# One PSUM pool of eight named banks for a whole retention-and-pooling trunk, in place of pools opened and closed by each stage

## The chip, the core and the metric

The kernel runs on one core of a Trainium2 chip. TensorE (PE in the profile) multiplies matrices and leaves its sums in PSUM, which has eight banks of 512 fp32 columns by 128 partitions here. VectorE (DVE) and ScalarE (ACT) read PSUM and work in SBUF, GpSimd (POOL) does little in this kernel, and SyncE (SP) issues the weight transfers. The metric is the device time of one execution in microseconds (us): the median of three runs.

## The reference, cut to what matters

The trunk has two layers on a sequence of 256 tokens of width 2048, both of the form h + layer(rms_norm(h)), and a last RMS norm.

```
def retention_layer(x, g_norm, w_in, gn, w_out):        # layer 0
    p = rms_norm(x, g_norm) @ w_in                       # 2048 -> 12288
    q, k, v, z = jnp.split(p, [...], axis=-1)            # 8 heads, 256 / 256 / 512 / 512 wide
    q, k = rope(q), rope(k) * 256 ** -0.5
    o = chunkwise_retention(q, k, v)                     # causal, decayed, chunks of 128
    o = group_norm_per_head(o) * gn * jax.nn.silu(z)
    return o @ w_out                                     # 4096 -> 2048

def pooling_layer(x, g_norm, w_in, w_grp, b_grp, scale, w_out):   # layer 1
    u, z = jnp.split(rms_norm(x, g_norm) @ w_in, [4096], axis=-1) # 2048 -> 8192
    mix = causal_window_mean(u, windows=(2, 4, 8, 16)) - u        # 4 groups of 1024
    mix = (einsum('bsgc,gcd->bsgd', mix, w_grp) + b_grp) * scale
    return (mix * jax.nn.silu(z)) @ w_out                         # 4096 -> 2048
```

## The kernel before

All matrices are fp32, and every product is made of three: each operand is cut into a high part (a cast by ACT, line 91) and a low part (source minus high, by DVE, line 92), and TensorE sums high x high, high x low and low x high. A transfer brings one unit of weights (1 MB, tag `raw`, three buffers); `weights` cuts it into two pairs (tag `w`, five buffers), each pair with a high and a low half of 1024 columns.

The work falls into four stages, one after the other in the program:

- the **first stage** (lines 186 to 353), retention: eight heads with four groups for q and k (`acc`), scores (`sc`), v (`accv`), outputs (`po`), a column sum (`tot`) and four groups for the gate (`acc`, then `gz`). A group of `stationary` is 16 pairs of matmuls, line 122 (512 columns) and line 123 (256 columns). `joined` adds the two halves of the bank (ACT copy, line 131, DVE add, line 132);
- **way 1** (lines 387 to 479, called at line 518), the output projection of retention: for each half of the columns 16 units of weights go into eight sums in eight banks, `c11` to `c22` and the Strassen products `p1`, `p5`, `p6`, `p7`. The four units at the start of a half are plain ones (24 matmuls of line 363 each), so the first Strassen unit comes after 96 matmuls `c`. The last sums are added to the residual `xn` (line 408), and `turn` transposes the new columns by TensorE (`turned`, line 510) and cuts them into `hs2` (lines 96 and 97) for the next stage;
- the **second stage** (lines 551 to 598), pooling: for each of four windows eight groups for u, eight for the gate (`acc` from `hs2`) and eight half groups with `pool_grp` (`acc` from `ms`), each of the latter read by ACT (line 590) and DVE (line 592) and cut into `gs`. At its start `spread_norm` makes the norm's reciprocal on DVE (lines 147 to 163 and 534) and spreads it with two matmuls `tot` (line 139);
- **way 2** (line 645), the output projection of pooling, as way 1 but with the last norm as its tail.

A list scheduler sets the order of the instructions on each engine; it sees which tile holds which bank. Each engine then runs its instructions in that order, and waits at the front one. In the kernel before, each stage opens its own PSUM pools and closes them at its end:

```
        with tc.tile_pool(name=f"{name}_acc", bufs=3, space=bass.MemoryType.PSUM) as acc:
            with tc.tile_pool(name=f"{name}_ret", bufs=5, space=bass.MemoryType.PSUM) as rest:
```

The first and the second stage take three banks for `acc` and five for the rest; each of way 1 and way 2 takes a pool of eight tags, one per sum. A pool that opens gets banks of the pools that were closed, and its first tile comes after the last reading of their tiles.

Of the kernel before, what the change touches and what calls it, by code (L numbers as in the profile page):

```python
# [7 lines left out]
F32 = mybir.dt.float32  # L8
# [5 lines left out]
P = 128  # L14
D = 2048
S = 256
# [14 lines left out]
CLASSIC = ((0, 0), (0, 1), (1, 0), (2, 0), (3, 0), (1, 1), (4, 0), (5, 0), (2, 1), (3, 1), (4, 1), (5, 1))  # L31
FIRST = (20, 16)


# [11 lines left out]
def kernel(  # L46
# [30 lines left out]
    ev = ctx.enter_context(tc.tile_pool(name="ev", bufs=2))  # L77
    psum = []

    @contextmanager  # L80
    def banks(name):

        with tc.tile_pool(name=f"{name}_acc", bufs=3, space=bass.MemoryType.PSUM) as acc:
            with tc.tile_pool(name=f"{name}_ret", bufs=5, space=bass.MemoryType.PSUM) as rest:
                psum[:] = acc, rest
                yield

# [46 lines left out]
    def column_sums(sums):  # L134

        sp = ev.tile([P, 2, S], F32R, tag="sp", name="sp", bufs=1)
        split(sp[:, 0], sp[:, 1], sums)
        tot = psum[1].tile([P, 512], F32, tag="ret", name="tot")
        nc.tensor.matmul(tot[:, :S], ones, sp[:, 0], start=True, stop=False)
        nc.tensor.matmul(tot[:, :S], ones, sp[:, 1], start=False, stop=True)  # L140
        return tot[:, :S]
# [42 lines left out]


    with banks("first"), tc.tile_pool(name="rt", bufs=1) as rt:

        cold = psum[1].tile([P, 512], F32, tag="ret", name="cold")
        for _ in range(9):
# [5 lines left out]
        qk = rt.tile([P, 4, S], F32, tag="qk", name="qk")  # L195
        accs = [psum[0].tile([P, 512], F32, tag="acc", name="acc") for _ in range(3)]
        accs.append(psum[1].tile([P, 512], F32, tag="ret", name="acc"))
        for u in range(4):
# [7 lines left out]
            for i in range(2):  # L206
# [33 lines left out]
        nc.vector.tensor_tensor(out=rpr, in0=rp, in1=wide(rs, 2), op=ALU.mult)  # L240
        rst = psum[1].tile([P, 512], F32, tag="ret", name="rst")
        rsn = rt.tile([P, 2], F32, name="rsn")
# [4 lines left out]
        os = act.tile([P, VT, 2, S], F32R, tag="os", name="os")  # L247
        unit = 4
        for h in range(NH):
# [3 lines left out]
            for c in range(4 if h else 0):  # L253
                blocks = blocks_of(weights(ret_in[unit]))
                unit += 1
                acc = psum[0].tile([P, 512], F32, tag="acc", name="acc")
                stationary(acc, blocks, hs)
                joined(qk[:, c], acc)
# [12 lines left out]
            tc.keep_in_program_order(nc.gpsimd.dma_start(out=mk, in_=masks[h]))  # L271
            sc = psum[1].tile([P, 2, S], F32, tag="ret", name="sc")
            n = 0
# [4 lines left out]
            n = 0  # L278
# [12 lines left out]

            accv = [psum[0].tile([P, 512], F32, tag="acc", name="accv") for _ in range(2)]
            for c in range(4):
# [24 lines left out]
            for c in range(4):  # L318
                cs = slice(c * P, (c + 1) * P)
                po = psum[1].tile([P, 512], F32, tag="ret", name="po")  # L320
# [17 lines left out]
            for c in range(4):  # L338
                blocks = blocks_of(weights(ret_in[unit]))
                unit += 1  # L340
                acc = psum[0].tile([P, 512], F32, tag="acc", name="acc")
# [13 lines left out]
    class Sum:  # L355


        def __init__(self, pool, name, n):
            self.tile, self.n, self.done = pool.tile([P, 512], F32, tag=name, name=name), n, 0

# [25 lines left out]

    def way_out(A, src, first, forms, tmp, pool, work, order, y, after, ends=False):

# [7 lines left out]
        for p in range(2):  # L396
            plain = len(CLASSIC) // 2 * 12
            sums = {}
            for name in order:
                n = 0 if name == "c22" else 3 * NS  # L400
                sums[name] = Sum(pool, name, n + (plain if name[0] == "c" else 0))
            out_of = {(t, c): sums[f"c{t + 1}{c + 1}"] for t in range(2) for c in range(2)}
# [14 lines left out]
            for n, kind in enumerate(ORDER):  # L417
# [16 lines left out]
                b = raw.rearrange("p (m f) -> p m f", m=4)  # L434
# [46 lines left out]
    with tc.tile_pool(name="pl", bufs=1) as pl:  # L481
# [8 lines left out]

        with (
            tc.tile_pool(name="way1", bufs=1, space=bass.MemoryType.PSUM) as way,
            tc.tile_pool(name="work1", bufs=1) as work,
        ):
# [45 lines left out]
        gs = act.tile([P, VT, 2, S], F32R, tag="os", name="gs")  # L540
# [10 lines left out]
        for g, win in enumerate(WINDOWS):  # L551
# [3 lines left out]
            for c in range(GT):  # L555
                blocks = blocks_of(weights(pool_in[2 * GT * g + c]))
                acc = psum[0].tile([P, 512], F32, tag="acc", name="acc")
                stationary(acc, blocks, hs2)
# [17 lines left out]
            for c in range(GT):  # L576
                blocks = blocks_of(weights(pool_in[2 * GT * g + GT + c]))
                acc = psum[0].tile([P, 512], F32, tag="acc", name="acc")
                stationary(acc, blocks, hs2)
                joined(gz[:, c], acc)  # L580
                nc.vector.tensor_tensor(out=gz[:, c], in0=gz[:, c], in1=rs, op=ALU.mult)
                nc.scalar.activation(gz[:, c], gz[:, c], AF.Silu)
            for c in range(GT // 2):
                halves = weights(pool_grp[GT // 2 * g + c])
                for i in range(2):
                    e = GT * g + 2 * c + i
                    acc = psum[0].tile([P, 512], F32, tag="acc", name="acc")
                    stationary(acc, blocks_of(halves[i : i + 1]), ms)
# [48 lines left out]

        with (
            tc.tile_pool(name="way2", bufs=1, space=bass.MemoryType.PSUM) as way,
            tc.tile_pool(name="work2", bufs=1) as work,  # L640
        ):
            tmp = act.tile([P, 4 * S + 2 * P + 512], F32, tag="hs", name="tmp")
            forms = pl.tile([P, NS, 4, 2, P], F32R, tag="ms", name="forms")
            order = ("p1", "p5", "p6", "c11", "c21", "c12", "c22", "p7")
            way_out(gs, pool_out, FIRST[1], forms, tmp, way, work, order, stream, norm, True)

# [110 lines left out]
```

## Time and profile before

| | before |
|---|---|
| median of three runs | 1393.86 us (1393.78 to 1394.25) |
| the profiled execution | 1391.64 us |
| its span | 1389.5 us |
| PE busy | 1364.1 us, 98% of the span |
| DVE busy | 1060.9 us, 76% |
| ACT busy | 719.7 us, 52% |
| POOL busy | 25.4 us, 2% |
| mean granted TensorE clock | 0.99 of full speed |

The profile is that of one execution; its span runs from the first to the last instruction, and the execution's own time is 2.1 us longer. Busy times are those of the engine's instructions. The starts of the rows are what a sum of work can be read from, since matmuls overlap each other and the duration of one is longer than the distance to the next. The stages can be told apart by the tile names: the first stage ends at 576.5 us, way 1 runs from 577.6 to 751 us, the second stage from 755.7 to 1202.7 us, and way 2 from 1207.5 us.

### The profile page before, as it was taken

The numbers are of one execution on the slowest core, as the hardware profiler recorded it, in microseconds if no ns is written. First come the engines' busy times: TensorE is split into PE (matmuls) and PEld (weight loads), VectorE is DVE, ScalarE is ACT, GpSimd is POOL, SyncE is SP. The second block draws the span as 40 slices with busy tenths as digits, with TensorE's granted clock in tenths as the row PEclk, the third lists the DMA queues.
The fourth block names the chain that finished last, engine by engine and source line by source line (L and its number), as shares of the span: only waits on it lengthen the run. The fifth ranks groups of instructions, "written<-read, shape, count | busy, mean of one in ns | idle before, by whom it ended". The sixth has DMA issues, their size and how long they took to land.

```text
span 1389.5 us, 18380 instructions
## 1 busy us (share of the span) xinstructions
PE 1364.1 (98%) x7176; PEld 1171.6 (84%) x7176; DVE 1060.9 (76%) x1545; ACT 719.7 (52%) x1027; POOL 25.4 (2%) x33
## 2 busy tenths in 40 slices
PE   8999999999999999999998999999999999899997
PEld 7888888888888888888887888888888888788885
DVE  6886868686868686898777867876886896868676
ACT  6455545455545454555454455455545545545443
POOL 0000000000000000000000000000000000000102
PEclk8999999999999999999999999999999999999999
DMA  8545454545555545475555555555555555446552
GB/s 298 209 161 197 172 191 177 190 179 188 182 187 180 184 173 190 153 261 196 182 189 180 195 199 182 185 199 195 183 188 191 198 185 185 179 164 230 182 210 93
DMA packets 39493, 262.66 MB, mean 189 GB/s; under 512 B 4512, under 2 KB 4896, under 8 KB 9072
## 3 DMA queue, kind: packets, MB, share of 16 engines
q1 hardware_dynamic: 37872, 255.93, 52.0%
q0 software_dynamic: 1536, 5.57, 1.1%
q8 instruction: 56, 0.92, 0.3%
q14 instruction: 29, 0.24, 0.0%
HBM read 259.39 MB, written 2.10 MB: 188 GB/s over the span
## 4 chain that ended last, share of the span: by engine, by line
PE 96%; DVE 2%; ACT 1%; issue 1%; DMA 1%; SPq 0%; DVEq 0%; ACTq 0%
PE acc L122 37%; PE c L363 21%; PE acc L123 19%; PE accv L302 4%; PE accv L304 4%; PE accv L303 4%; PE p L363 3%; PE po L322 1%; DVE w L92 1%; DMA xin<-in_xT 1%; PE po L324 1%; PE sc L276 0%; DVE hs L97 0%; PE sc L281 0%; ACT w L91 0%
## 5 line engine op out<-in xcount | busy, mean ns | idle before, releaser
L92 DVE TENSOR_TENSOR w<-raw,w 128x1024 fp32r<-128x1024 f32 x472 | 568.1, 1209 | 168.0 <-ACT w L91 160.0
L122 PE MATMUL acc<-hs,w 128*128 128x512 f32 x1984 | 692.4, 392 | 3.5 <-DVE rs_t L161 3.5
L91 ACT CAST w<-raw 128x1024 fp32r<-128x1024 f32 x472 | 486.9, 1038 | 305.0 <-PE acc L123 130.7
L123 PE MATMUL acc<-hs,w 128*128 128x256 f32 x1984 | 556.1, 280 | 0.0
L122 PEld LDWEIGHTS acc<-hs,w 128*128 128x128 f32 x1984 | 372.0, 187 | 84.7 <-issue 3.7
L123 PEld LDWEIGHTS acc<-hs,w 128*128 128x128 f32 x1984 | 375.5, 189 | 1.0
L363 PE MATMUL c<-w,gs 128*128 128x512 f32 x624 | 149.3, 394 | 4.6 <-DVE m L592 4.6
L131 ACT COPY hl<-acc 128x256 f32<-128x256 f32 x128 | 47.9, 374 | 199.5 <-PE acc L123 197.0
L363 PE MATMUL c<-w,os 128*128 128x512 f32 x624 | 149.3, 391 | 0.9 <-DVE gz L132 0.9
L363 PEld LDWEIGHTS c<-w,gs 128*128 128x128 f32 x624 | 118.7, 190 | 30.6 <-issue 4.9
L363 PEld LDWEIGHTS c<-w,os 128*128 128x128 f32 x624 | 116.6, 188 | 26.1 <-DVE gz L132 1.2
L302 PE MATMUL accv<-w,hs 128*128 128x512 f32 x256 | 99.8, 390 | 1.2 <-DVE qk L132 1.2
L303 PE MATMUL accv<-w,hs 128*128 128x512 f32 x256 | 99.8, 390 | 0.0
L304 PE MATMUL accv<-w,hs 128*128 128x512 f32 x256 | 99.7, 390 | 0.0
L122 PE MATMUL acc<-ms,w 128*128 128x512 f32 x256 | 90.6, 397 | 0.0
L123 PE MATMUL acc<-ms,w 128*128 128x256 f32 x256 | 72.0, 281 | 0.0
L91 ACT CAST w<-s 128x1024 fp32r<-128x1024 f32 x32 | 33.6, 1050 | 52.0 <-PE c L363 43.9
L122 PEld LDWEIGHTS acc<-ms,w 128*128 128x128 f32 x256 | 48.1, 188 | 11.8
L92 DVE TENSOR_TENSOR w<-s,w 128x1024 fp32r<-128x1024 f32 x32 | 39.2, 1224 | 24.4 <-ACT w L91 24.4
L302 PEld LDWEIGHTS accv<-w,hs 128*128 128x128 f32 x256 | 48.1, 188 | 11.1 <-DVE qk L132 1.5
L304 PEld LDWEIGHTS accv<-w,hs 128*128 128x128 f32 x256 | 48.0, 188 | 10.1
L303 PEld LDWEIGHTS accv<-w,hs 128*128 128x128 f32 x256 | 48.1, 188 | 9.7
(159 smaller groups left out, 1052.7 us busy)
## 6 DMA issues: line engine op xcount, KB each, us to landing
raw<-in_ret_in SPq DMA_DIRECT2D x92, 1024.0 KB, 4.9
raw<-in_pool_in SPq DMA_DIRECT2D x64, 1024.0 KB, 4.9
raw<-in_ret_out SPq DMA_DIRECT2D x32, 1024.0 KB, 4.9
raw<-in_pool_out SPq DMA_DIRECT2D x32, 1024.0 KB, 4.9
raw<-in_pool_grp SPq DMA_DIRECT2D x16, 1024.0 KB, 4.9
xin<-in_ret_in SPq DMA_DIRECT2D x7, 512.0 KB, 8.5
xn<-in_xN POOLq DMA_DIRECT2D x4, 512.0 KB, 6.9
out<-xn SPq DMA_DIRECT2D x8, 256.0 KB, 2.3
```

Source lines behind the costliest of these rows:

```text
L91: nc.scalar.copy(hi, src)
L92: nc.vector.tensor_tensor(out=lo, in0=src, in1=hi.bitcast(F32), op=ALU.subtract)
L122: nc.tensor.matmul(acc, hi, moving[:, k], start=(k == 0), stop=False)
L123: nc.tensor.matmul(acc[:, :S], lo, moving[:, k, 0], start=False, stop=(k == n - 1))
L131: nc.scalar.copy(t, acc[:, S:])
L302: nc.tensor.matmul(accv[t], hs[:, k, 0, ts], hi[:, ws], start=(k == 0), stop=False)
L303: nc.tensor.matmul(accv[t], hs[:, k, 0, ts], lo[:, ws], start=False, stop=False)
L304: nc.tensor.matmul(accv[t], hs[:, k, 1, ts], hi[:, ws], start=False, stop=(k == KT - 1))
L322: nc.tensor.matmul(po[:, :S], vs[:, 0, p, cs], ss[:, q, :S], start=(n == 0), stop=(n == 2))
L324: nc.tensor.matmul(po[:, S:], vs[:, 1, p, cs], ss[:, :, S:], start=(p == 0), stop=(p == 1))
L363: nc.tensor.matmul(self.tile, a, w, start=(self.done == 0), stop=(self.done == self.n - 1))
```

## The change

One pool holds eight tiles, with the tags `b0` to `b7`, for the whole kernel. `bank(i, name)` takes a tile of bank i; `ring("acc", ...)` hands out b0 to b2 in turn, `ring("ret", ...)` b3 to b7, and the turns go on from stage to stage. The sums of way 1 and way 2 have fixed banks, in the order of `SUMS`; in way 1 the order was another. The transposed tiles take banks 0 and 1, or 2 and 7. A tile now waits only for the last reading of the tile that held its own bank.

```diff
+SUMS = ("p1", "p5", "p6", "c11", "c21", "c12", "c22", "p7")
...
-    psum = []
-
-    @contextmanager
-    def banks(name):
-
-        with tc.tile_pool(name=f"{name}_acc", bufs=3, space=bass.MemoryType.PSUM) as acc:
-            with tc.tile_pool(name=f"{name}_ret", bufs=5, space=bass.MemoryType.PSUM) as rest:
-                psum[:] = acc, rest
-                yield
+    psum = ctx.enter_context(tc.tile_pool(name="psum", bufs=1, space=bass.MemoryType.PSUM))
+    turns = {"acc": 0, "ret": 0}
+
+    def bank(i, name):
+        return psum.tile([P, 512], F32, tag=f"b{i}", name=name)
+
+    def ring(kind, name):
+
+        start, n = (0, 3) if kind == "acc" else (3, 5)
+        turns[kind] += 1
+        return bank(start + (turns[kind] - 1) % n, name)
...
-        tot = psum[1].tile([P, 512], F32, tag="ret", name="tot")
+        tot = ring("ret", "tot")
...
-            self.tile, self.n, self.done = pool.tile([P, 512], F32, tag=name, name=name), n, 0
+            self.tile, self.n, self.done = bank(i, name), n, 0
...
-                    turned = way.tile([P, 512], F32, tag=(("p1", "p5"), ("p6", "p7"))[c % 2][i], name="turned")
+                    turned = bank(((0, 1), (2, 7))[c % 2][i], "turned")
...
-            order = ("p1", "p5", "p6", "p7", "c11", "c21", "c12", "c22")
-            way_out(os, ret_out, FIRST[0], forms, tmp, way, work, order, stream, turn)
+            way_out(os, ret_out, FIRST[0], forms, tmp, work, stream, turn)
         second = ctx.enter_context(ExitStack())
-        second.enter_context(banks("second"))
```

The number of instructions on each engine is the same, and so is the order on SP and POOL. The order moves on PE, DVE and ACT around the three places where a stage follows another, and a little in the first two heads (there the column sum `tot` and the scores `sc` of a head stand some twelve to fourteen matmuls later, and two gate groups change places). In the changed kernel the helpers' line numbers are higher by three (122 is 125, 97 is 100, 363 is 366).

From way 1 to the second stage TensorE's queue read as follows before (`c_5641` and `c_5642` are the last sums of way 1, c12 and c22; `hs_4997` is `hs2`):

```order
L363 MATMUL c_5642<-w,os 128x512 x6
L363 MATMUL c_5641<-w,os 128x512 x12
L363 MATMUL c_5642<-w,os 128x512 x12
L510 MATMUL turned<-idt,xn 128x128 x8
L122 MATMUL acc<-hs_4997,w 128x512
L123 MATMUL acc<-hs_4997,w 128x256
```

With the change, 13 matmuls of the first group (`acc_6265`) stand between the last `c` and the first two transposes, and after nine more it goes on like this (`w_6262` is the group's second pair of weights, `acc_6393` the second group):

```order
L126 MATMUL acc_6265<-hs2_4989,w_6262 128x256
L125 MATMUL acc_6265<-hs2_4989,w_6262 128x512
L126 MATMUL acc_6265<-hs2_4989,w_6262 128x256
L510 MATMUL turned_6220<-idt_300,xn_4982 128x128 x3
L510 MATMUL turned_6229<-idt_300,xn_4982 128x128 x3
L125 MATMUL acc_6265<-hs2_4989,w_6262 128x512
L126 MATMUL acc_6265<-hs2_4989,w_6262 128x256
L125 MATMUL acc_6393<-hs2_4989,w_6387 128x512
L126 MATMUL acc_6393<-hs2_4989,w_6387 128x256
```

So the eight transposes, which stood in one piece ahead of the second stage, now stand inside its first group; 12 of that group's 16 pairs come before the second group, and its last four, which need the last four blocks of `hs2`, come after eleven pairs of the second.

On DVE the same place read before (`a_6313` and `r_6316` belong to the norm's reciprocal):

```order
L92 TENSOR_TENSOR w<-raw,w 128x1024 x2
L528 TENSOR_REDUCE a_6313<-part_4988 128x2
L97 SCALAR_TENSOR_TENSOR hs_4997<-turned,vec,hs_4997 128x256 x2
L529 TENSOR_SCALAR a_6313<-a_6313 128x2
L147 TENSOR_SCALAR rs_t<-a_6313 128x2
L97 SCALAR_TENSOR_TENSOR hs_4997<-turned,vec,hs_4997 128x256
```

and reads with the change:

```order
L95 TENSOR_TENSOR w<-raw,w 128x1024 x2
L526 TENSOR_REDUCE a_6298<-part_4983 128x2
L527 TENSOR_SCALAR a_6298<-a_6298 128x2
L150 TENSOR_SCALAR rs_t<-a_6298 128x2
L153 TENSOR_SCALAR r_6301<-rs_t 128x2
L164 TENSOR_TENSOR rs_t<-r_6301 128x2
L95 TENSOR_TENSOR w<-raw,w 128x1024
L165 SCALAR_TENSOR_TENSOR rs_t<-rs_t,a_6298 128x2
L100 SCALAR_TENSOR_TENSOR hs_4989<-turned,vec,hs_4989 128x256 x2
```

The `w` that stands alone is the low half of the second group's second pair; it has moved ahead of the four last blocks of `hs2` (line 100), and behind five steps of the reciprocal.

From the second stage to way 2 TensorE's queue read before:

```order
L122 MATMUL acc<-ms,w 128x512
L123 MATMUL acc<-ms,w 128x256
L363 MATMUL c_10377<-w,gs 128x512 x12
L363 MATMUL c_10378<-w,gs 128x512 x12
L363 MATMUL c_10379<-w,gs 128x512 x12
```

With the change nine matmuls of way 2 stand ahead of the last two groups of the second stage, and the other 87 of its first 96 behind them:

```order
L366 MATMUL c_10357<-w,gs 128x512
L366 MATMUL c_10358<-w,gs 128x512
L366 MATMUL c_10357<-w,gs 128x512 x5
L366 MATMUL c_10358<-w,gs 128x512 x2
L125 MATMUL acc<-ms,w 128x512
L126 MATMUL acc<-ms,w 128x256
```

Here c11 (`c_10357`) and c21 (`c_10358`) take banks that no `acc` has used, so their first matmuls need weights and old blocks of `gs` alone.

## Rows read from the trace of the kernel before

**Rows 1.** The page: busy time of the engines, share of the span, instructions.

```profile
PE 1364.1 (98%) x7176; PEld 1171.6 (84%) x7176; DVE 1060.9 (76%) x1545; ACT 719.7 (52%) x1027; POOL 25.4 (2%) x33
```

**Rows 2.** Waits of PE: line, what was waited for, us in total, times, longest.

```profile
PE c L363 <- DVE m L592: 4.6, 1, 4.6
...
PE acc L122 <- DVE rs_t L161: 3.5, 1, 3.5
PE accv L302 <- DVE qk L132: 1.2, 1, 1.2
...
PE c L363 <- DVE gz L132: 0.9, 1, 0.9
```

**Rows 3.** Timeline of PE, first stage to way 1: start, duration, line, tiles, count.

```profile
576.20 0.39 PE L122 MATMUL acc<-hs,w 128*128 128x512 f32 x1
576.43 0.28 PE L123 MATMUL acc<-hs,w 128*128 128x256 f32 x1
577.63 22.04 PE L363 MATMUL c<-w,os 128*128 128x512 f32 x96 [0.92 <-DVE gz L132]
599.51 0.84 PE L363 MATMUL p<-w,os 128*128 128x512 f32 x3
600.19 0.85 PE L363 MATMUL c<-w,os 128*128 128x512 f32 x3
```

**Rows 4.** Timeline of DVE, first stage to way 1.

```profile
577.15 0.42 DVE L132 TENSOR_TENSOR gz<-acc,hl 128x256 f32<-128x256 f32 x1 [0.17 <-ACT hl L131]
```

**Rows 5.** Timeline of PE, way 1 to the second stage.

```profile
742.91 0.82 PE L510 MATMUL turned<-idt,xn 128*128 128x128 f32 x6
743.48 7.09 PE L363 MATMUL c<-w,os 128*128 128x512 f32 x30
750.41 0.38 PE L510 MATMUL turned<-idt,xn 128*128 128x128 f32 x2
751.35 0.88 PE L510 MATMUL turned<-idt,xn 128*128 128x128 f32 x6 [0.56 <-DVE xn L408]
755.69 0.77 PE L122 MATMUL acc<-hs,w 128*128 128x512 f32 x1 [3.46 <-DVE rs_t L161]
...
759.51 0.39 PE L122 MATMUL acc<-hs,w 128*128 128x512 f32 x1
...
759.86 0.39 PE L122 MATMUL acc<-hs,w 128*128 128x512 f32 x1
...
762.63 0.28 PE L139 MATMUL tot<-sp,ones 128*128 128x256 f32 x1
```

**Rows 6.** Timeline of DVE, way 1 to the second stage.

```profile
750.61 0.69 DVE L408 TENSOR_TENSOR xn<-xn,c 128x512 f32<-128x512 f32 x1 [1.72 <-PE c L363]
751.21 2.35 DVE L92 TENSOR_TENSOR w<-raw,w 128x1024 fp32r<-128x1024 f32 x2
...
755.07 0.48 DVE L97 SCALAR_TENSOR_TENSOR hs<-turned,vec,hs 128x256 fp32r<-128x256 f32 x1
```

**Rows 7.** Timeline of ACT, way 1 to the second stage.

```profile
749.60 2.05 ACT L91 CAST w<-raw 128x1024 fp32r<-128x1024 f32 x2
```

**Rows 8.** Timeline of PE, second stage to way 2.

```profile
1202.63 0.28 PE L123 MATMUL acc<-ms,w 128*128 128x256 f32 x1
1207.55 24.35 PE L363 MATMUL c<-w,gs 128*128 128x512 f32 x96 [4.64 <-DVE m L592]
```

**Rows 9.** Timeline of DVE, second stage to way 2.

```profile
1206.92 0.48 DVE L592 SCALAR_TENSOR_TENSOR m<-acc,vec,hl 128x256 f32<-128x256 f32 x1
```

**Rows 10.** Windows: stretch, length, busy PE, PEld, DVE, ACT, POOL, granted clock, DMA.

```profile
577.60:599.68 22.08, 22.05 (x97) 18.29 (x98) 21.15 (x32) 9.39 (x12) 2.85 (x4) 1.00 0.64 224
...
756.00:758.00 2.00, 2.00 (x7) 1.71 (x7) 1.45 (x9) 0.27 (x1) 0.00 (x0) 0.50 0.27 111
...
1205.00:1210.00 5.00, 2.45 (x6) 2.00 (x7) 5.00 (x11) 1.44 (x4) 0.54 (x1) 0.57 0.36 149
...
1207.50:1232.00 24.50, 24.45 (x98) 20.04 (x99) 15.84 (x24) 9.32 (x14) 0.54 (x1) 0.90 0.50 172
```

More of the change, by code (lines that the diff above doesn't have):

```diff
@@ L1 @@
-from contextlib import ExitStack, contextmanager
+from contextlib import ExitStack
 import concourse.bass as bass
@@ L183 @@
     hs = act.tile([P, KT, 2, S], F32R, tag="hs", name="hs")
-    with banks("first"), tc.tile_pool(name="rt", bufs=1) as rt:
-        cold = psum[1].tile([P, 512], F32, tag="ret", name="cold")
+    with tc.tile_pool(name="rt", bufs=1) as rt:
+        cold = ring("ret", "cold")
         for _ in range(9):
@@ L195 @@
         qk = rt.tile([P, 4, S], F32, tag="qk", name="qk")
-        accs = [psum[0].tile([P, 512], F32, tag="acc", name="acc") for _ in range(3)]
-        accs.append(psum[1].tile([P, 512], F32, tag="ret", name="acc"))
+        accs = [ring("acc", "acc") for _ in range(3)]
+        accs.append(ring("ret", "acc"))
         for u in range(4):
@@ L240 @@
         nc.vector.tensor_tensor(out=rpr, in0=rp, in1=wide(rs, 2), op=ALU.mult)
-        rst = psum[1].tile([P, 512], F32, tag="ret", name="rst")
+        rst = ring("ret", "rst")
         rsn = rt.tile([P, 2], F32, name="rsn")
@@ L255 @@
                 unit += 1
-                acc = psum[0].tile([P, 512], F32, tag="acc", name="acc")
+                acc = ring("acc", "acc")
                 stationary(acc, blocks, hs)
@@ L271 @@
             tc.keep_in_program_order(nc.gpsimd.dma_start(out=mk, in_=masks[h]))
-            sc = psum[1].tile([P, 2, S], F32, tag="ret", name="sc")
+            sc = ring("ret", "sc").rearrange("p (m s) -> p m s", s=S)
             n = 0
@@ L289 @@
             split(ss[:, 0], ss[:, 1], sm)
-            accv = [psum[0].tile([P, 512], F32, tag="acc", name="accv") for _ in range(2)]
+            accv = [ring("acc", "accv") for _ in range(2)]
             for c in range(4):
@@ L319 @@
                 cs = slice(c * P, (c + 1) * P)
-                po = psum[1].tile([P, 512], F32, tag="ret", name="po")
+                po = ring("ret", "po")
                 for n, (p, q) in enumerate(((0, 0), (0, 1), (1, 0))):
@@ L340 @@
                 unit += 1
-                acc = psum[0].tile([P, 512], F32, tag="acc", name="acc")
+                acc = ring("acc", "acc")
                 stationary(acc, blocks, hs)
@@ L355, with __init__ @@
     class Sum:
-        def __init__(self, pool, name, n):
-            self.tile, self.n, self.done = pool.tile([P, 512], F32, tag=name, name=name), n, 0
+        def __init__(self, i, name, n):
+            self.tile, self.n, self.done = bank(i, name), n, 0
         def add(self, a_hi, a_lo, w_hi, w_lo):
@@ L385, in sides, with way_out @@
         put(3, s)
-    def way_out(A, src, first, forms, tmp, pool, work, order, y, after, ends=False):
+    def way_out(A, src, first, forms, tmp, work, y, after, ends=False):
         def blk(k, t):
@@ L398, in way_out @@
             sums = {}
-            for name in order:
+            for i, name in enumerate(SUMS):
                 n = 0 if name == "c22" else 3 * NS
-                sums[name] = Sum(pool, name, n + (plain if name[0] == "c" else 0))
+                sums[name] = Sum(i, name, n + (plain if name[0] == "c" else 0))
             out_of = {(t, c): sums[f"c{t + 1}{c + 1}"] for t in range(2) for c in range(2)}
@@ L489, in stream @@
             return xn[:, :, cs] if t is None else xn[:, t, cs]
[L491 to L494, printed above, removed]
+        with tc.tile_pool(name="work1", bufs=1) as work:
             tmp = pl.tile([P, 4 * S + 2 * P + 512], F32, tag="gz", name="tmp")
@@ L556 @@
                 blocks = blocks_of(weights(pool_in[2 * GT * g + c]))
-                acc = psum[0].tile([P, 512], F32, tag="acc", name="acc")
+                acc = ring("acc", "acc")
                 stationary(acc, blocks, hs2)
@@ L577 @@
                 blocks = blocks_of(weights(pool_in[2 * GT * g + GT + c]))
-                acc = psum[0].tile([P, 512], F32, tag="acc", name="acc")
+                acc = ring("acc", "acc")
                 stationary(acc, blocks, hs2)
@@ L586 @@
                     e = GT * g + 2 * c + i
-                    acc = psum[0].tile([P, 512], F32, tag="acc", name="acc")
+                    acc = ring("acc", "acc")
                     stationary(acc, blocks_of(halves[i : i + 1]), ms)
@@ L636, in norm @@
                 nc.sync.dma_start(out=out[t][:, ps], in_=piece)
[L638 to L641, printed above, removed]
+        with tc.tile_pool(name="work2", bufs=1) as work:
             tmp = act.tile([P, 4 * S + 2 * P + 512], F32, tag="hs", name="tmp")
             forms = pl.tile([P, NS, 4, 2, P], F32R, tag="ms", name="forms")
-            order = ("p1", "p5", "p6", "c11", "c21", "c12", "c22", "p7")
-            way_out(gs, pool_out, FIRST[1], forms, tmp, way, work, order, stream, norm, True)
+            way_out(gs, pool_out, FIRST[1], forms, tmp, work, stream, norm, True)
 def _layout(inputs):
```

## The prediction, made before the changed kernel ran

> **What bounds the kernel now.** I read the page first. TensorE is busy 98% of the span, DVE 76%, ACT 52% [rows 1]. An engine that is busy all the time leaves little to win except its own waits, so the second view is the list of PE's waits [rows 2]. Over a microsecond there are, behind the loading at the start (which the change doesn't touch), three, and each has one place only: 4.6 us of line 363, 3.5 us of line 122 and 1.2 us of `accv`; another of 0.9 us belongs to line 363 too. The third view, the timeline of PE, tells where: the waits of line 363 stand at the first matmul of way 1 [rows 3] and at that of way 2 [rows 8], the one of line 122 at the first matmul of the second stage [rows 5]. These three are the seams between stages, where pools close and open; the 1.2 us of `accv` are inside the first head. The windows tell the rest: behind the two longer waits the granted clock stood at 0.50 and 0.57 of full speed [rows 10], so these seams cost more than their waits.
>
> **Seam 1, first stage to way 1.** The last matmul of line 123 starts at 576.43; the next after such a one starts 0.12 later (a pair is 0.35 long by [rows 5], 0.23 of it between lines 122 and 123 by [rows 3]). Way 1 starts at 577.63, so 577.63 - 576.55 = 1.08 us are lost. What it waited for ended at 577.15 + 0.42: DVE's reading of the last `acc` [rows 4]. With the change the first tile, c11, is in bank 3, which was read long before, and the wait goes. How much of it stays gone is set by DVE, which makes the operands of the first Strassen unit at 599.5. In the 22.08 us of these 96 matmuls it is busy 21.15 [rows 10], idle 0.93. If all that work were needed at their end, PE could come no more than 0.9 earlier. Bounds 0 and 1.08; I take 0.9, since that window shows idle time of this size and no row a wait at 599.51.
>
> **Seam 2, way 1 to the second stage.** From the first two transposes at 750.41 to `tot` at 762.63 there are 12.22 us, for eight transposes and 16 pairs [rows 5]. At full speed a pair takes 759.86 - 759.51 = 0.35 us (0.347 over the nine pairs from 759.51 to `tot`), 16 take 5.55; six transposes took 743.48 - 742.91 = 0.57, eight 0.76. So 12.22 - 6.31 = 5.9 us are lost: the wait of 0.56 before the transposes, the 3.46 before the first `acc`, and the clock. (The releaser named for the 3.46 is a step of the reciprocal; what ends then is the last reading of `turned` by line 97, at 755.07 + 0.48 [rows 6].) The seven pairs from 755.69 to 759.51 took 3.82, where 2.43 is full speed, so the clock's part is 1.4.
>
> With the change the first group starts behind the last `c`, at about 750.4 in the old time. I walked the new order along durations from the rows. Thirteen matmuls of `acc` take 2.3, so the first transposes come at 752.7; they need `xn`, the second half of which is written at 750.61 + 0.69 = 751.30 [rows 6]. The wait of 0.56 is covered. The tightest place is the second group's second pair of weights. Its buffer is read out by the first group's eighth pair, at 750.4 + 8 x 0.347 + 0.2 (two transposes) = 753.4; ACT's cast takes 1.03 (two took 2.05 [rows 7]), to 754.5. The low half is DVE's: behind two such halves, 751.21 to 753.56 [rows 6], and five short steps, then 1.2 us of its own, to about 755.8. PE wants it after four more pairs, six transposes and eight pairs: 753.4 + 1.4 + 0.6 + 2.8 = 758.2. The margin is 2.4 us. The last four blocks of `hs2` follow on DVE and are wanted later still, which is what the new order pays for by putting eleven pairs of the second group ahead. So I forecast no wait here and no fall of the clock: 5.9 us. Bounds: nothing, if the wait only moves, and 5.9.
>
> **Seam 3, second stage to way 2.** The last `acc` matmul starts at 1202.63, so way 2 could start at 1202.75; it starts at 1207.55 [rows 8], when line 592 has read the last `acc` at 1206.92 + 0.48 [rows 9]. That is 4.8 us. DVE was late there since it was fully busy (5.00 of 5 us [rows 10]) with work for way 2 that stood ahead of it. The first 96 matmuls then took 24.35, where the same 96 took 22.04 in way 1 at full clock [rows 3, 8]: 2.3 more. Sum 7.1 us. With the change c11 and c21 stand in banks that the second stage's `acc` never had, and nine of their matmuls even run two groups earlier; those nine are moved, not saved. What could take the gain back is DVE, which must still make the `forms` and sums for the first Strassen unit, now wanted 7.1 us sooner. In the 24.5 us up to that unit it is busy 15.84 [rows 10], idle 8.66, and that is more than 7.1. Bounds: nothing and 7.1; I take 7.1.
>
> **What costs nothing.** The number of instructions and transfers is unchanged, as is the order of SP and POOL; no queue of transfers is passed by anything. A ring of three and one of five hold as many tiles as the two pools did, so inside the stages a tile's bank comes free as many tiles later as before. The 1.2 us of `accv` in head 0 wait for a bank in that ring of three, and stay. The moves in the first two heads (`tot` and `sc` some twelve to fourteen matmuls later) lie where PE has other groups to run; were this cover missing, one wait would cost about what that one row shows, 1.2 us.
>
> **Sum.** 0.9 + 5.9 + 7.1 = 13.9 us. The profiled execution took 1391.64; so the changed one should take 1377.7, with a span near 1375.6. The median before, 1393.86, lies 2.2 above the profiled execution; against it the forecast is 1393.86 - 13.9 = **1380.0 us**.
>
> **The rivals.**
> (a) The seam 2 wait comes back elsewhere. For it: the second group's weights go through DVE, which runs the reciprocal's steps in the same queue, and the margin of 2.4 us is the smallest of my walk. If PE stalls there, the clock may fall again as it did after 3.46 us. Half to all of 5.9 is lost: 1383 to 1386. Against it: DVE had 0.55 us idle in the 2 us from 756 [rows 10].
> (b) DVE becomes the bound of way 2's beginning. For it: it is at 5.00 of 5 us across the seam. If its work can't be moved up, PE waits at the first Strassen unit, and of 7.1 us up to all is lost: 1383 to 1387. Against it: 8.66 us of idle time, of which 7.1 are used. The point from which it decides is 1.6 us of DVE work more than I count.
> (c) The change doesn't do what it says: the scheduler orders by its own model, and a stage's first tile could still wait for the last one's readers. Then it is 1393 to 1394. Against it: c11 stands in bank 3, and nine of its matmuls run before the last two `acc` groups.
> (d) Slower: the fixed ring makes PE wait for a bank in every head, as the 1.2 us of `accv` in head 0 do. Eight such waits are 9.6 us and would leave a gain of 4.3 (1389.6); from 13.9 / 8 = 1.7 us per head there is no gain, from 2.1 it is slower by over 0.2%. At 2.5 us it would be 1400. Against it: in the rings as many tiles lie between two uses of a bank as before, and no other head shows such a wait [rows 2].
> (e) Changing banks more often costs clock. Were it so, the some 23 pairs of the interleaved part of seam 2 would run at half speed, as the seven pairs above did, and cost 23 x 0.3 = 7 us: 1387. Against it: from 599.51 way 1 changes banks every three matmuls, and three take 600.19 - 599.51 = 0.68, or 0.23 each, as in the 96 before them [rows 3].
>
> The Trainium skill has a rule that speaks for (e): the page "TensorE: Matmul & The Clock Gate", section "A second HAM failure mode: psum-queue depth-cycling", tells of a kernel in which cycling through PSUM banks left TensorE idle for moments so often that its clock went down and up again. By that rule the interleaved groups could run at the lower of the two clocks; this case's trace doesn't agree as far as way 1 goes, whose banks change at 0.23 us per matmul.
>
> **How the numbers follow.** The forecast, all three seams run through, has 0.70, and by itself reaches from 1379 to 1382. (a) has 0.11, (b) 0.08, (e) 0.02, (c) 0.03 and (d) 0.04; the rest, 0.02, is for a gain beyond it. The low end is the sum with all bounds, 14.1, and a run's spread of some 0.5 on either side: 1393.86 - 14.1 - 0.5 gives 1379.2, and I take 1378.5. The high end takes in (a) and (b): 1387. About 0.2% (2.8 us) is what a measurement of this kernel can tell from no change. Faster than that: the forecast, (a), (b), (e) and the rest, a little taken off for mixtures: 0.91. Same 0.05, slower 0.04.
>
> **What the profile after would show.** PE's waits: no wait of over half a microsecond at the first `c` of either way, none of 3 us at the first `acc` of the second stage; `accv` with its 1.2 as before. The 96 matmuls of way 2's beginning at 0.23 us each with clock 1.00, and no window under 0.9 near 745 to 760 or 1190 to 1215. Way 1's start 1 us after the last group's pair goes to 0.1. PE's busy time falls by some 3.7 us, the two clock parts (1.4 and 2.3), and the idle part by some 10. The prediction is wrong if a wait for DVE's `w` shows at the second group of the second stage, for `forms` or `w` at the first Strassen unit of a way, or for a bank inside heads.

## The result

The changed kernel took 1378.97 us (median of four runs, 1378.28 to 1379.07), the kernel before beside it 1394.05 us (1393.78 to 1394.55): 15.1 us less, a ratio of 0.989 with a 95% interval from 0.9873 to 0.9907. Measured again later, beside other kernels, it took 1379.75 us against 1393.92 us, 14.2 us less, 0.9899 (0.9884 to 0.9914). The forecast was 1380.0 us. The profiled execution took 1379.03 us with a span of 1377.0 us, 12.5 us under the span of before.

The page after, its busy line, answers to [rows 1]:

```profile
PE 1361.7 (99%) x7176; PEld 1168.6 (85%) x7176; DVE 1059.1 (77%) x1545; ACT 719.0 (52%) x1027; POOL 25.4 (2%) x33
```

The waits of PE after (line, what was waited for, us in total, times, longest) answer to [rows 2]:

```profile
PE acc L224 <- ACT w L94: 4.2, 3, 2.2
PE cold L193 <- POOL ones_f L183: 1.0, 1, 1.0
PE accv L305 <- DVE qk L135: 0.6, 1, 0.6
```

All the waits at the seams are gone: the 4.6 and 0.9 us of the first `c` of either way, the 3.5 us of the first `acc` of the second stage and the 0.6 us ahead of the transposes. What is left stands at the start, in the first 40 us. The timeline of PE after at the three seams answers to [rows 3, 5, 8] (start, duration, line, tiles, count):

```profile
576.63 0.28 PE L126 MATMUL acc<-hs,w 128*128 128x256 f32 x1
576.75 21.96 PE L366 MATMUL c<-w,os 128*128 128x512 f32 x96
598.55 0.84 PE L366 MATMUL p<-w,os 128*128 128x512 f32 x3
...
742.47 7.07 PE L366 MATMUL c<-w,os 128*128 128x512 f32 x30
749.38 0.39 PE L125 MATMUL acc<-hs,w 128*128 128x512 f32 x1
...
751.73 0.38 PE L510 MATMUL turned<-idt,xn 128*128 128x128 f32 x2
...
753.48 0.82 PE L510 MATMUL turned<-idt,xn 128*128 128x128 f32 x6
...
755.89 0.40 PE L125 MATMUL acc<-hs,w 128*128 128x512 f32 x1
...
757.54 0.28 PE L126 MATMUL acc<-hs,w 128*128 128x256 f32 x1
...
1191.75 2.25 PE L366 MATMUL c<-w,gs 128*128 128x512 f32 x9
1199.48 19.91 PE L366 MATMUL c<-w,gs 128*128 128x512 f32 x87
1219.23 0.85 PE L366 MATMUL p<-w,gs 128*128 128x512 f32 x3
```

Read the starts. At seam 1 the first `c` starts 0.12 us behind the last matmul of the stage before, as any matmul of that kind does; at seam 2 the first `acc` starts where the transposes stood, and these now lie inside the group; at seam 3 nine `c` run ahead of the last two groups, and the other 87 follow the last group at once (1199.48). The windows after (columns as in [rows 10]) show what the clock did:

```profile
756.00:758.00 2.00, 2.00 (x13) 1.72 (x12) 1.86 (x10) 0.75 (x2) 0.00 (x0) 1.00 0.74 258
...
1201.00:1206.00 5.00, 5.00 (x24) 4.14 (x23) 5.00 (x8) 3.29 (x5) 0.53 (x1) 1.00 0.88 331
1206.00:1211.00 5.00, 5.00 (x24) 4.14 (x23) 5.00 (x8) 2.40 (x3) 0.00 (x0) 1.00 0.74 274
```

The granted clock is 1.00 in both places that stood at 0.50 and 0.57 before, and PE is busy in all of these windows. So it is from 742 to 762 us, which takes in the whole interleaved stretch: busy for 20.00 of 20 us, clock 1.00.

**Where the 12.5 us between the two profiled spans lie.** From stretches of the timelines, before minus after: up to the last group of the first stage 576.55 - 576.75 = -0.20; the gap of seam 1, 1.08 - 0.00 = 1.08; way 1 up to its last `c`, 172.78 - 172.63 = 0.15; seam 2, the stretch with 16 pairs and eight transposes, 12.22 - (755.89 - 749.38) = 5.71; the rest of the second stage, 440.12 - (1199.48 - 755.89 - 9 x 0.229) = -1.41; seam 3, up to the first Strassen unit, 28.99 - (1219.23 - 1199.48 + 9 x 0.229) = 7.18; the rest -0.01. The seams give 13.97, against 13.9 in the forecast. The -1.41 was in no case of the prediction; the last section tells of it.

### The profile page after: what moved, and what is told of

It is laid out like the page before. It is cut to its first block, busy times and chain, and to the rows that moved or that the text cites. A ratio compares the mean times of both kernels' runs of the same rounds, so it can differ in the third digit from the quotient of the medians.

```text
span 1377.0 us, 18376 instructions
## 1 busy us (share of the span) xinstructions
PE 1361.7 (99%) x7176; PEld 1168.6 (85%) x7176; DVE 1059.1 (77%) x1545; ACT 719.0 (52%) x1027; POOL 25.4 (2%) x33
## 4 chain that ended last, share of the span: by engine, by line
PE 97%; DVE 1%; ACT 1%; issue 1%; DMA 1%; SPq 0%; DVEq 0%; ACTq 0%
PE acc L125 37%; PE c L366 21%; PE acc L126 19%; PE accv L305 4%; PE accv L307 4%; PE accv L306 4%; PE p L366 3%; PE po L325 1%; PE po L327 1%; DMA xin<-in_xT 1%; PE sc L279 0%; DVE w L95 0%; ACT w L94 0%; PE sc L284 0%; PE turned L510 0%
```

## The experiments

### The seams one at a time, and none

Four kernels have the named banks and the rings of the change, but close the pool and open a new one at some of the seams. `no_seam` does so at all three, the others at all but the one they are named after.

```diff
+    def reopen_banks(name):
+        psum[1].close()
+        open_banks(name)
...
+    reopen_banks("psum_way1")
     with tc.tile_pool(name="pl", bufs=1) as pl:
...
+        reopen_banks("psum_second")
         second = ctx.enter_context(ExitStack())
...
         second.close()
+        reopen_banks("psum_way2")
```

Expected of `no_seam`: 

> All three seams closed again: the pool of eight named banks is closed and a new one opened between the stages, so only the named banks and the rings inside the stages are left of the change. Theory (the gain is at the seams alone): the time of before within 1 us, 1393 to 1395 us, with the three waits of PE back (about 1, 3.5 and 4.6 us). Rival (the rings or the other order of the banks help or harm inside the stages): over 2 us away from before, without a change of these waits.

Measured: 1392.75 us against 1392.78 us, 0.9999 (0.9991 to 1.0008). The waits of PE in its profile are those of [rows 2] at every seam:

```profile
...
PE c L376 <- DVE m L602: 4.6, 1, 4.6
PE acc L135 <- DVE rs_t L174: 3.5, 1, 3.5
PE accv L315 <- DVE qk L145: 2.5, 1, 2.5
PE cold L203 <- POOL ones_f L193: 1.0, 1, 1.0
PE c L376 <- DVE gz L145: 0.9, 1, 0.9
PE turned L521 <- DVE xn L421: 0.6, 1, 0.6
```

So the names, the rings and the other order of the sums in way 1 are worth nothing by themselves that these runs can tell (the interval is 1.2 us on either side); the gain lies at the seams.

Expected of `seam1_only`: 

> One pool for the first stage and way 1, new pools at the other two seams. Theory: 0.9 to 1.1 us less than before, the wait of 0.9 us at the first matmul of way 1 gone, no fall of the clock there before or after. Rival (DVE gives the operands of the first Strassen unit at the same time as before, so PE waits there instead): no gain, and a wait of about 1 us at 598 to 600 us.

Measured: 1392.41 us, 1.000 (0.9991 to 1.0009), too little for the runs to tell. Its trace tells: the first `c` of way 1 starts at 576.74, right behind the last group, and the first Strassen unit follows without a wait.

```profile
576.74 21.96 PE L376 MATMUL c<-w,os 128*128 128x512 f32 x96
598.54 0.84 PE L376 MATMUL p<-w,os 128*128 128x512 f32 x3
```

The 1.08 us are gone there, and none comes back at 598 to 600 us.

Expected of `seam2_only`: 

> One pool for way 1 and the second stage, new pools at the other two seams. Theory: the wait of 3.5 us and the half clock behind it go, 5.9 us less than before by the trace around the seam. Rival (what the trace of the whole change shows further on is part of it: pairs of matmuls at 0.353 us in place of 0.347 in some hundred us of the second stage): 4.3 us less, with such a stretch again in the second stage.

Measured: 1387.82 us, 0.9963 (0.995 to 0.9975), 5.0 us less. Both expectations lie inside the interval. In the trace the wait and the half clock are gone, and slow pairs stand in the second window, as in the changed kernel. The stretch of 16 pairs and eight transposes takes 6.51 us, as in the changed kernel, where before took 12.22. From the end of way 1's `c` (750.26) to that of the stage's last group (1198.28) it takes 448.02 us where before took 452.34, 4.3 us less: the rival's account, the seam's gain less a slow stretch, is borne out by the trace.

Expected of `seam3_only`: 

> One pool for the second stage and way 2, new pools at the other two seams. Theory: 4.8 us of wait and 2.3 us of half clock, 7.1 us less than before. Rival (runs without change spend more at this seam than the profiled execution showed, since the measured gain of the whole change is 15.1 and the profiled executions differ by 12.6): 8 us or more.

Measured: 1386.79 us, 0.9946 (0.9932 to 0.9959), 6.0 us less, with a slow stretch in the first window this time. The theory's 7.1 is inside the interval (5.7 to 9.5 us), and so is the rival's 8. The trace decides: it has the nine early matmuls, no wait and clock 1.00, and the seam's stretch is 7.2 us shorter than before, as in the changed kernel.

```profile
1199.42 2.25 PE L376 MATMUL c<-w,gs 128*128 128x512 f32 x9
...
1207.15 19.91 PE L376 MATMUL c<-w,gs 128*128 128x512 f32 x87
1226.89 0.85 PE L376 MATMUL p<-w,gs 128*128 128x512 f32 x3
```

The three medians add up to 11.3 us, less than the 14 to 15 of the whole; but each has an interval of plus and minus one to two microseconds, so the runs neither bear out nor refute that the three add up. The stretches of the traces do: 1.1, 5.7 and 7.2 us, each as in the whole change.

### Does the clock fall because PE is idle?

At seam 3 the prediction put 4.8 us to the wait and 2.3 us to the clock. Two kernels take the kernel before, and put 18 matmuls into its gap, in a bank that is free there; what they sum is not used.

```diff
+        fill = psum[1].tile([P, 512], F32, tag="ret", name="fill")
+        for _ in range(18):
+            nc.tensor.matmul(fill, gs[:, VT - 2, 0, :P], gs[:, VT - 2], start=True, stop=True)
         second.close()
```

Expected of `filled_gap3`: 

> The kernel before, with 18 matmuls of 512 columns in a free bank that keep TensorE at work during the wait between the second stage and way 2 (they need a block of gs that is written some 0.4 us after the stage's last matmul; their sum is not used). Theory (4.8 us of that seam are the wait and 2.3 us the half clock behind it): the first c of way 2 starts as late as before, the clock stays at 1.00, its first 96 matmuls take 22.0 us in place of 24.3, and the kernel is 2.3 us faster than before. Rival (the half clock comes from something else in the seam than the idle time): the 96 matmuls take 24 us again, time as before.

Measured: 1397.04 us, 1.0024 (1.0014 to 1.0034): slower. The block that I had chosen is written not 0.4 but 3.9 us after the last group, so the gap stayed and the fillers came behind it. The timeline of PE:

```profile
1208.33 6.00 PE L602 MATMUL fill<-gs 128*128 128x512 f32 x18 [3.82 <-DVE gs L92]
1214.38 22.10 PE L363 MATMUL c<-w,gs 128*128 128x512 f32 x96
```

Eighteen matmuls took 6.00 where the next kernel's took 4.38: they paid for the fall of the clock, and the 96 behind them ran in 22.10. So this run is no test of the idle time. `filled_gap3b` has `VT - 3` in place of `VT - 2`, a block that is written earlier.

Expected of `filled_gap3b`: 

> As the filled gap, but the 18 matmuls need a block of gs that is written one group earlier, about 0.4 us after the stage's last matmul. Theory (2.3 us of the seam are the clock's, which falls since TensorE is idle): they start within 0.5 us of the last acc, all at 0.23 us and clock 1.00, the first c comes as late as before (4.8 us behind the last acc), its 96 take 22.0 us, and the span up to the first Strassen unit is 2.3 us shorter than before. Rival: a fall of the clock remains, 24 us for the 96.

Measured: 1391.40 us, 0.9986 (0.9977 to 0.9996). The timeline and a window:

```profile
1205.75 4.38 PE L602 MATMUL fill<-gs 128*128 128x512 f32 x18 [0.24 <-DVE gs L92]
1210.24 22.04 PE L363 MATMUL c<-w,gs 128*128 128x512 f32 x96
...
1205.00:1210.00 5.00, 4.76 (x22) 3.48 (x20) 4.86 (x12) 2.65 (x6) 0.00 (x0) 1.00 0.62 210
```

The first `c` comes as late as before (4.9 us behind the last group, which ended at 1205.35), but the clock stood at 1.00 and the 96 matmuls took 22.04 us where they took 24.35 [rows 8]. From the last group to the first Strassen unit it is 26.8 us in place of 29.0. So 2.2 to 2.3 us of this seam are the clock's, and the idle time is what brought it down. By the medians the kernel is 1.2 us faster (0.6 to 3.2 by the interval); a slow stretch of pairs in its first window, of which the last section tells, stands against the 2.3.

The Trainium skill says as much on its page "TensorE: Matmul & The Clock Gate", section "HAM oscillation — how this bites in real kernels": a wait between bursts of matmuls lets the engine drop to half its clock, so the next burst starts cold. This case's traces agree, with 0.50 and 0.57 behind the waits and 1.00 where fillers stood in the gap.

### How much can VectorE be late at seam 3?

```diff
+        for _ in range(more):
+            nc.vector.tensor_scalar(out=a, in0=a, scalar1=1.0, scalar2=None, op0=ALU.mult)
...
-                        sides(A, first, n // 2, tmp, forms)
+                        sides(A, first, n // 2, tmp, forms, MORE if ends and p == 0 and n == 3 else 0)
```

with MORE = 6, in the changed kernel. The call that gets them makes operands for the third and the fourth Strassen unit; in VectorE's queue it stands ahead of the first.

Expected of `dve_late3`: 

> The changed kernel, with six more operations of 128x1024 on VectorE (a multiplication by one, about 1.2 us each, some 7 us) among the work for the first Strassen units of way 2. Theory of the prediction (VectorE has 1.6 us to spare up to the first Strassen unit, behind that it is the bound): a wait of 4 to 6 us of PE for VectorE at the Strassen units from about 1219 us on, the kernel some 5 us slower than the changed one, or more with a fall of the clock. Rival (VectorE has much more slack, since the operands of a unit are wanted one after the other and the plain units behind it give time): no wait over 1 us, the time of the changed kernel within 1 us.

Measured: 1379.45 us, 0.9898 (0.9883 to 0.9913), the time of the changed kernel. The six took 0.7 us each and not 1.2, so 4.1 us and not 7 were added; five of them began ahead of the first Strassen unit, which starts at 1218.68. DVE in its trace (one of the six) and the window:

```profile
1211.90 0.68 DVE L378 TENSOR_SCALAR tmp<-tmp 128x1024 f32<-128x1024 f32 x1
...
1216.00:1221.00 5.00, 5.00 (x24) 4.10 (x23) 4.97 (x7) 2.84 (x3) 0.00 (x0) 1.00 0.30 125
```

PE waited nowhere there: the window has it busy in all 5.00 us, with DVE at 4.97. But this does not test the prediction's point of decision, 1.6 us more of DVE work ahead of the first unit. The scheduler put seven short operations of the same call (lines 95 and 381 to 387 of the changed kernel) behind that unit, so from the last group to the unit DVE was busy 18.70 of 19.74 us, where the changed kernel has 18.20 of 19.75: 0.5 us more. What the run does show is the rival's account: work that is counted up to the first unit can be done behind it without a wait of PE. How much more work it would take to make PE wait stays open.

### Is it the choice of banks?

```diff
-SUMS = ("p1", "p5", "p6", "c11", "c21", "c12", "c22", "p7")
+SUMS = ("c11", "c21", "c12", "p1", "p5", "p6", "c22", "p7")
```

Expected of `sums_swapped`: 

> The changed kernel with other banks for the sums: c11, c21 and c12 in banks 0 to 2, which the acc ring uses, p1, p5 and p6 in 3 to 5. The last acc of the first and of the second stage lies in bank 0, as c11 does here. Theory (one pool alone gives nothing at seams 1 and 3; the gain comes from first sums in banks that the stage before has left for long): the waits of 1.1 and 4.8 us and the half clock behind the latter are back, seam 2 stays as in the changed kernel, 8 us slower than that, about 1388 us. Rival (the closing and opening of pools costs, wherever the sums lie): the time of the changed kernel within 1 us.

Measured: 1380.14 us, 0.9909 (0.9894 to 0.9924). My theory fell, and the rival's time came. The first `c` of way 2 starts in its trace at 1197.99, behind the last group at once, although bank 0, that of c11, is read 4.2 us later:

```profile
1197.99 21.99 PE L366 MATMUL c<-w,gs 128*128 128x512 f32 x96
1219.82 0.85 PE L366 MATMUL p<-w,gs 128*128 128x512 f32 x3
```

```profile
1202.17 0.48 DVE L590 SCALAR_TENSOR_TENSOR m<-acc,vec,hl 128x256 f32<-128x256 f32 x1
```

The order of TensorE's queue says why: the scheduler starts way 2 with c22, then c21 and c12, and takes up c11 only after 40 matmuls.

```
L366 MATMUL c22_10360<-w_10396,gs_6243 128x512 x6
L366 MATMUL c21_10355<-w_10364,gs_6243 128x512 x6
L366 MATMUL c21_10355<-w_10367,gs_6243 128x512 x6
L366 MATMUL c22_10360<-w_10399,gs_6243 128x512 x6
L366 MATMUL c12_10356<-w_10396,gs_6243 128x512 x6
```

So the bank of a sum hardly matters, as long as some sum has a free one: with a dependency for each bank the scheduler can order the sums around the one that is late. Opening a pool takes that choice away, since all of its tiles wait: in `no_seam`, where the sums have the same banks as in the changed kernel, the 4.6 us were back.

### The two kernels once more

Expected of `after_again`: 

> The changed kernel unaltered, on the same chip as the kernels beside it. Theory (14.0 us are saved at the seams, and what two executions differ by beyond that is a stretch of one window of the second stage in which a pair of matmuls takes 0.353 us in place of 0.347, some 1.7 us each, in any execution of either kernel): 13 to 15 us less than before by the medians, and the slow stretch at another place or absent in this profile. Rival (the change itself puts that stretch there, in the second window from 868 us): the stretch at 868 to 969 us again, 12.3 us less than before by the profiled spans.

Measured: 1379.75 us, 0.9899 (0.9884 to 0.9914), 14.2 us less. Its profile has the slow stretch in the second window again, from 863 us. So the theory is right on the time and wrong on the stretch, for which the rival is right.

Expected of `before_again`: 

> The kernel before unaltered, one more profile. Theory: the waits at the seams as in the first profile (4.8, 3.5 and 1.1 us), the loading at the start and the place of the slow stretch (pairs at 0.353 us) different. Rival: the same profile to within 0.2 us, without a slow stretch outside the groups with pool_grp.

Measured: 1393.48 us, span 1391.4 us. The waits of PE:

```profile
PE c L363 <- DVE m L592: 4.6, 1, 4.6
PE acc L221 <- ACT w L91: 4.1, 2, 2.4
PE acc L122 <- DVE rs_t L161: 3.5, 1, 3.5
PE accv L302 <- DVE qk L132: 2.5, 1, 2.5
...
```

The waits at the seams are the same to 0.1 us. The start isn't: `accv` waits 2.5 us in place of 1.2, the granted clock falls behind that wait (0.70 from 35 to 40 us, where the first profile has 1.00), and the first stage ends at 577.85 in place of 576.55 us. Outside the groups with `pool_grp` no pairs are slow in the second stage of either profile of before.

### A wait that was left

The one bank wait left in the changed kernel is that of the first head's `accv`. In `accv_free` these two tiles take banks 3 and 5, and the ring of five is moved on by that.

```diff
+        accv0 = [bank(3, "accv"), bank(5, "accv")]
+        turns["ret"] = 3
...
+            if h == 0:
+                turns["ret"] = 6
             sc = ring("ret", "sc")
...
-            accv = [ring("acc", "accv") for _ in range(2)]
+            accv = [ring("acc", "accv") for _ in range(2)] if h else accv0
```

Expected of `accv_free`: 

> The changed kernel, with the two accv tiles of the first head in banks 3 and 5 in place of the next two of the acc ring, and the ring of five moved on by that, so that they need not wait for the reading of the first acc tiles. Theory (the wait of 0.5 to 2.5 us of accv in the first head is for a bank alone): that wait is gone and the kernel 0.5 to 2.5 us faster than the changed one, about 1378 us. Rival (VectorE is full from 30 to 40 us, so PE then waits for weights instead): a wait for w of the same length, the same time.

Measured: 1375.05 us (1373.99 to 1376.07) against 1392.59 us, 0.9874 (0.9858 to 0.9891). That is 17.5 us less than before, and the fastest kernel of this study; beside the changed kernel's 0.989 and 0.9899 it is some 2 to 5 us better by the medians. Its waits of PE, all of them:

```profile
PE acc L226 <- ACT w L94: 3.3, 2, 1.7
PE cold L193 <- POOL ones_f L183: 1.0, 1, 1.0
```

The first `accv` starts at 33.21 us, 3.6 us earlier than at 36.80 in the changed kernel:

```profile
33.21 0.63 PE L309 MATMUL accv<-w,hs 128*128 128x512 f32 x2
```

```profile
36.80 0.50 PE L305 MATMUL accv<-w,hs 128*128 128x512 f32 x1 [0.58 <-DVE qk L135]
```

and the first stage ends at 572.82 where it ended at 576.75. That is more than the wait of 0.58 that the profile named, and by the medians the gain is more than the theory gave. Part of it is the start: in this execution the granted clock stood at 1.00 from 5 to 20 us, where the changed kernel's first profile has 0.88, 0.50 and 0.60 in the three windows of 5 us, so the matmuls `acc` ahead of `accv` were done 2.85 us earlier (the last starts at 33.09 in place of 35.94). `after_again`, the changed kernel with 1.00 from 5 to 20 us, shows what such a start is worth while the wait is there:

```profile
36.69 0.79 PE L305 MATMUL accv<-w,hs 128*128 128x512 f32 x1 [2.54 <-DVE qk L135]
37.29 0.63 PE L306 MATMUL accv<-w,hs 128*128 128x512 f32 x1
```

Its last `acc` starts at 33.88, but VectorE reads the banks hardly sooner (from 36.22 us, in the first profile from 36.33): PE waits 2.54 us, the clock falls (0.66 from 35 to 40 us), and the first stage ends at 578.15. So this wait is a small seam, a gap and matmuls at half clock behind it, where the start is quick. The profile of `accv_free` has no slow stretch either, which gives another 1.3 us; how much of the gain would remain with one, no run shows.

## Why the prediction was right

**The time.** Forecast 1380.0, measured 1378.97 and 1379.75, and the mechanism (all three seams run through) is what the traces show: 13.97 us of the seams, forecast 13.9. That the time was met to 1.0 and 0.3 us is in part luck, since a loss of 1.41 us in the second stage was not foreseen and the intervals are two microseconds on either side.

**Seam 1** was sized at 0.9 and measured 1.08, the upper bound. The step that was off is the one from VectorE's idle time (0.93 us in that stretch) to what PE can gain: VectorE did not have to finish all its work of the stretch by the first Strassen unit. Between the last group and that unit it was busy 21.83 of 22.96 us before and 21.16 of 21.80 with the change, and no wait came at 598.55.

**Seam 2**, 5.9 forecast, 5.71 measured; 0.1 of the difference is that the 16 pairs took 0.353 us each and not 0.347. The walk held up well. The low half of the second group's second pair, for which it gave 755.8 and a margin of 2.4 us, was this row of DVE in the changed kernel; less the 1.0 us by which everything stands earlier, the forecast is 754.8:

```profile
753.70 1.23 DVE L95 TENSOR_TENSOR w<-raw,w 128x1024 fp32r<-128x1024 f32 x1 [0.28 <-ACT w L94]
```

It ended at 754.93, and PE took it up at 757.54: a margin of 2.6 us. Rival (a) didn't come.

**Seam 3**, 7.1 forecast, 7.18 measured; the split into wait and clock is shown by `filled_gap3b`. Rival (b) didn't come: PE took up the first Strassen unit at 1219.23 without a wait. Its 8.66 us of idle time less 7.1 are what VectorE had left (1.55 us idle up to that unit), but not all of the slack: work for the third and the fourth unit stood among the 18.20 us that it did, and `dve_late3` has seven operations of it behind the first unit, without a wait. What the slack is, no run shows.

**What costs nothing.** `no_seam` shows it, at 0.9999, to 1.2 us: rings and named banks inside the stages. Rivals (c) and (d) fall with the absence of waits. Rival (e) falls with the windows: where the transposes stand among the `acc` matmuls, the clock is 1.00. So the rule on cycling through PSUM banks (Trainium skill, "TensorE: Matmul & The Clock Gate", section "A second HAM failure mode: psum-queue depth-cycling") does not show in this kernel: from 742 to 762 us PE is busy throughout.

**What was missed.** PE's busy time was to fall by 3.7 us, the two clock parts; it fell by 2.4 (1364.1 to 1361.7). The difference of 1.3 is about what the slow stretch of the second stage costs, which the profiled spans show (12.5 in place of 13.9) and the medians, with intervals of two microseconds on either side, do not. That `accv` keeps its 1.2 us was wrong in the number: it was 0.6, and over all profiles with this wait 0.5 to 2.5, as the start goes. Nor did the prediction, which set this wait aside as one of 1.2 us, see that the clock can fall behind it too.

## What to carry to other kernels

In this kernel a pool that closed and opened between stages made the next stage's first tile wait for the slowest reader of the last one, at all three seams; a tag for each bank over the whole kernel gives one wait for each bank, and a scheduler that can then order the work around the one that is late. Price such a seam as the gap and the matmuls at half clock behind it, both read off the starts in the timeline, and walk the new order with durations from rows to find the tightest operand. When a wait of the same kind remains somewhere, look there next, and in more than one profile: one that was 0.6 us in the first profile was 2.5 us and a fall of the clock in the second.

## What was not expected of the hardware

A pair of matmuls of 512 and 256 columns took either 0.347 or 0.353 us in the second stage, with the granted clock at 1.00 in both, and all pairs of a block took the same: the 256 pairs for u and the gate of a window, or the 64 of its half groups with `pool_grp`. (Where seam 2 is joined, the some 30 pairs of the interleaved first groups, up to 761 us, took 0.353 too.) Before, the pairs of `pool_grp` took 0.353 in all four windows and the others 0.347. In the changed kernel the 256 of the second window (862 to 952 us) took 0.353, and the 64 of the first window's `pool_grp` 0.347: 256 x 0.0066 less 64 x 0.0064 is 1.3 us, nearly all of the 1.41 that the second stage lost; the rest is the end of the interleaved pairs. PE's instructions in 20 us show it. Of before, in the first and the second window:

```profile
780.00:800.00 20.00, 20.00 (x118) 17.62 (x117) 17.26 (x30) 10.26 (x16) 0.00 (x0) 1.00 0.60 209
...
900.00:920.00 20.00, 20.00 (x118) 17.62 (x117) 17.78 (x33) 9.68 (x15) 0.54 (x1) 1.00 0.53 178
```

Of the changed kernel, in the second:

```profile
900.00:920.00 20.00, 20.00 (x115) 17.36 (x114) 15.96 (x28) 9.94 (x16) 0.54 (x1) 1.00 0.53 175
```

Of `no_seam`, in the first:

```profile
780.00:800.00 20.00, 20.00 (x115) 17.35 (x114) 16.57 (x29) 9.39 (x15) 0.00 (x0) 1.00 0.49 166
```

The same work at 115 or at 118 instructions in 20 us. In the blocks of 256 pairs it is the matmul of 512 columns that grows, from 0.230 to 0.237 us from its start to the next, while that of 256 keeps 0.117; in those of `pool_grp` both grow, to 0.234 and 0.119. In 13 profiles the 256 slow pairs stood in the second window in all five that have seam 2 joined and the first head as it was (the changed kernel twice, `dve_late3`, `seam2_only`, `sums_swapped`), in the first window in `no_seam`, `seam3_only` and both filled kernels, and nowhere in the two profiles of before, `seam1_only` and `accv_free`. So it seems to go with the program and not with the execution. But up to seam 3 the filled kernels issue the same instructions in the same order as before, which has no such stretch, so the order alone doesn't set it; what does stays open.

The start varies from one execution to the next: in the first 20 us the granted clock fell to 0.50 in some profiles and stayed at 1.00 in others. The first `accv` came between 36.0 and 37.0 us all the same, in all twelve profiles in which it waits for VectorE. So the quick start gained nothing there, and lost: in the four profiles with the wait of 2.5 us (both second ones, `no_seam`, `filled_gap3b`) the clock stood at 0.66 to 0.70 from 35 to 40 us and the first stage ended between 577.3 and 578.2 us, in the eight others between 576.2 and 576.9.
